# Both heads' scores in one tile of two PSUM banks, in a three-layer transformer kernel

## The chip, the cores and the metric

The kernel runs on one core of a Trainium2 chip. The metric is device time in microseconds. The engines are PE (matrix products; PEld is its weight load), DVE (vector), ACT (activation function), POOL (general) and SP (here only DMA issue). PSUM, into which PE writes, has eight banks of 128 x 512 fp32 values.

## The reference

The sequence has 512 positions of 1024 channels, fp32 throughout. `reference()` runs one hybrid layer and then two further layers:

```python
# first layer: attention over a window of 128 with sinks, beside an RWKV7 recurrence
attn = sliding_window_sink_attention(q, k, v, rel_bias, sinks[l])
rw = rwkv7_time_mix(p, ...)                      # state per head, 64 x 64, step by step
x = x + rms_norm(concat([attn, rw]) @ w_out[l], ...)
x = x + rms_norm(conv_gated_ffn(...), ...)
# second layer (even): fox (scores plus a decay) and diff (p1 - lam * p2), 8 and 2 x 4 heads of 64
s = einsum('bqhd,bkhd->bhqk', qb, k) * scale + (cb[..., :, None] - c[..., None, :])
p = softmax(where(qpos[:, None] >= kpos[None, :], s, -inf))
# third layer (odd): dsa (an indexer picks the top 128 keys of each row) and stick-breaking attention
a = where(mask, exp(log_sigmoid(z) + after), 0.0)  # after: sums of log(1 - sigmoid) from the right
# each layer ends with a gated FFN with a short convolution
```

## The kernel before, in words

Activations stay on the chip, channels on partitions. A dense projection is one PSUM tile of 128 x 512. Every weight tile and every input is split into a high and a low part, and a product takes three matmuls for each 128 input channels (lines 222 to 224), 24 in a row for 1024 channels. `Stream` brings the weights by DMA from SP in units of 512 KB, and ACT and DVE split them (lines 335, 336).

The program has six stages: the first mixer (0 to about 440 us), its FFN (to 985), the even layer (to 1290), its FFN (to 1646), the odd layer (to 1946) and its FFN.

In the first mixer the string `CFG["order"]` lists the steps. D projects r, k and v of two heads, A makes the operands of the recurrence's chunks (lines 547 to 642: two low-rank products 553 and 560, then blocks of 64-row matmuls 620 and 621, transposes, and 638), I inverts a triangular system on DVE, J joins its quarters (683, 693), B runs the eight chunks one after the other (713 to 787), S is the window attention of one pair of heads (799 to 854), Q projects its queries, and F is the output projection. Each is there for j = 0 to 3. These chains share PE's queue with dense projections.

The order of instructions on an engine is made by a scheduler that places an instruction when its inputs and its buffers are free; the text order counts among those that share a buffer. A PSUM bank is taken with `bank(tag)` from a pool, new for each use: two of `q` (dense), two of `s`, one each of `b`, `n`, `a` and `o`. Dense tiles use `q`, and after the mixer (`spread`) every third one `b`. In the mixer A uses `s`, J and B use `b` (for j = 3 `s`), S uses `a`, and outputs of B and S collect in `o` or `n`. Later, transposes alternate between `n` and `a`, and scores use `s`.

In the even and odd layers a step is one pair of heads j and one block of 128 queries b, with n = 128 (b + 1) keys. Each head in turn takes a bank `s`, gets its score matmul (1130 in fox, 1169 in diff, 1302 in stick, 1327 in dsa) from one half of the 128 rows of the two heads' queries and keys, in fox a 32-row matmul for the decay (1131), and a mask added by a product with the identity. DVE reduces the maximum (1135, 1172, 1331), ACT exponentiates, PE transposes block by block (1000) into a bank that DVE or ACT copies out (1003, 1005), and `values` (1012) multiplies by v. In stick ACT takes two sigmoids, DVE scans and POOL multiplies (1309). The indexer's four heads (1248) are summed after a relu.

Of the kernel before, what the change touches and what calls it, by code (L numbers as in the profile page):

```python
# [22 lines left out]
P = 128  # L23
# [18 lines left out]
M3 = {"ot": 4, "pre": 2, "rtmp": 1, "isc": 3, "irl": 2, "selb": 3, "kf": 4, "vd": 4, "PT": 3,  # L42
      "sq": 1, "sk": 1, "svt": 2, "e": 4, "sg": 2, "sc": 2, "cq": 4, "w3": 3}
# [3 lines left out]
BANKS = dict(q=2, s=2, b=1, n=1, a=1, o=1)  # L47
# [18 lines left out]
class K:  # L66
    def __init__(self, tc, ctx, dbg):
        self.tc, self.nc, self.dbg = tc, tc.nc, dbg or {}
        self.c = ctx.enter_context(tc.tile_pool(name="cst", bufs=1))
        self.xp = ctx.enter_context(tc.tile_pool(name="xp", bufs=1))  # L70
        self.w = ctx.enter_context(tc.tile_pool(name="w", bufs=1))
        self.ps = ctx.enter_context(tc.tile_pool(name="ps", bufs=1, space=PSUM))
        self.dr = ctx.enter_context(tc.tile_pool(name="dr", bufs=1, space=DRAM))
        self.n = self.nq = self.nt = 0
        self.spread = False
# [18 lines left out]
    def bank(self, tag):  # L94
        self.n += 1
        return self.ps.tile([P, S], F32, name=f"{tag}_{self.n}", tag=tag, bufs=BANKS[tag])

    def psq(self):
        self.nq += 1
        return self.bank("b" if self.spread and self.nq % 3 == 0 else "q")  # L100

    def pss(self):
        return self.bank("s")

    def pstr(self, tag="tr"):
        if tag == "tr":
            self.nt += 1
            tag = "na"[self.nt % 2]
        return self.bank(tag)
# [341 lines left out]
def first_mixer(k, I):  # L451
# [51 lines left out]
    def swa_table():  # L503
# [3 lines left out]
        q = k.pstr("a")  # L507
# [473 lines left out]

def rows_T(k, p, b, i, tag="pT"):
    nc = k.nc
    q = k.pstr()
    for kb in range(b + 1):
        nc.tensor.transpose(q[:, kb * P:(kb + 1) * P], p[:, kb * P:(kb + 1) * P], k.ident)
    t = k.slot(tag)
    n = (b + 1) * P
    if i % 2:
        nc.vector.tensor_copy(t[:, :n], q[:, :n])  # L990
    else:
        nc.scalar.activation(t[:, :n], q[:, :n], AF.Copy)
    return t
# [49 lines left out]
def even_layer(k, I, x, h, st, bc, q):  # L1043
# [68 lines left out]
    def fox_proj(j):  # L1112
        qt = evac(k, k.proj(st, h), "aq", bc, 0.125)
        kt = evac(k, k.proj(st, h), "ak", bc)
# [3 lines left out]
    def fox(j, qt, kt, vt):  # L1118
        ls8 = k.small("ls8", 8)
        pts = [k.slot("PT", (P, 13, P)) for _ in range(2)]  # L1120
        for b in range(NB):
            for hh in range(2):
                hd = 2 * j + hh
                hs = slice(64 * hh, 64 * hh + 64)
                g, i = divmod(hd, 4)
                n = (b + 1) * P
                ex = [(CL[g][32 * i:32 * i + 32, b * P:(b + 1) * P], CR[g][32 * i:32 * i + 32, :n], 0),
                      (k.identb, k.causb, b * P)]
                q = k.pss()
                nc.tensor.matmul(q[:, :n], qt[hs, b * P:(b + 1) * P], kt[hs, :n], start=True, stop=False)  # L1130
                nc.tensor.matmul(q[:, :n], ex[0][0], ex[0][1], start=False, stop=False, tile_position=(32 * i, 0))
# [5 lines left out]
                nc.scalar.activation(p[:, :n], q[:, :n], AF.Exp, bias=nm, accum_out=ls8[:, u:u + 1])  # L1137
# [22 lines left out]
    def diff(j, qt, kt, vt):  # L1160
        ls1 = k.small("ls1", 4)
        o = k.pso()
        for b in range(NB):
            n = (b + 1) * P
            ps, l12 = [], k.small("l12", 2)
            for hh in range(2):
                hs = slice(64 * hh, 64 * hh + 64)
                q = k.pss()
                nc.tensor.matmul(q[:, :n], qt[hs, b * P:(b + 1) * P], kt[hs, :n], start=True, stop=False)  # L1169
                nc.tensor.matmul(q[:, b * P:n], k.identb, k.causb, start=False, stop=True)  # L1170
                nm = k.small("nm", 1)
                nc.vector.tensor_reduce(nm, q[:, :n], axis=AX.X, op=OP.max, negate=True)
                p = k.slot("p")
                nc.scalar.activation(p[:, :n], q[:, :n], AF.Exp, bias=nm,
# [32 lines left out]
    prev = None  # L1207
    for j in range(4):
        cur = fox_proj(j)
# [14 lines left out]
def odd_layer(k, I, x):  # L1224
# [17 lines left out]
    for b in range(1, NB):  # L1242
        n = (b + 1) * P
        sc = k.slot("isc")
        for i in range(4):
            hs = slice(64 * (i % 2), 64 * (i % 2) + 64)
            q = k.pss()
            nc.tensor.matmul(q[:, :n], iq[i // 2][hs, b * P:(b + 1) * P], ikd[hs, :n], start=True, stop=True)
            rl = k.slot("irl")
            nc.scalar.activation(rl[:, :n], q[:, :n], AF.Relu)  # L1250
            if i == 0:
                nc.vector.tensor_scalar(sc[:, :n], rl[:, :n], iw[:, 4 * b:4 * b + 1], None, op0=OP.mult)
            else:
                nc.vector.scalar_tensor_tensor(sc[:, :n], rl[:, :n], iw[:, 4 * b + i:4 * b + i + 1], sc[:, :n], op0=OP.mult, op1=OP.add)
# [40 lines left out]
    def stick(j, qt, kt, vt):  # L1295
        pts = [k.slot("PT", (P, 13, P)) for _ in range(2)]
        for b in range(NB):
            n = (b + 1) * P
            for hh in range(2):
                hs = slice(64 * hh, 64 * hh + 64)  # L1300
                q = k.pss()
                nc.tensor.matmul(q[:, :n], qt[hs, b * P:(b + 1) * P], kt[hs, :n], start=True, stop=False)
                nc.tensor.matmul(q[:, b * P:n], k.identb, k.strictb, start=False, stop=True)
                a, r = k.slot("e"), k.slot("sg")
                nc.scalar.activation(a[:, :n], q[:, :n], AF.Sigmoid)
                nc.scalar.activation(r[:, :n], q[:, :n], AF.Sigmoid, scale=-1.0)
                c = k.slot("sc")
                nc.vector.tensor_tensor_scan(c[:, n - 2::-1], r[:, n - 1:0:-1], r[:, n - 1:0:-1], 1.0, op0=OP.mult, op1=OP.min)  # L1308
                nc.gpsimd.tensor_tensor(a[:, :n - 1], a[:, :n - 1], c[:, :n - 1], op=OP.mult)
                u = 2 * b + hh  # L1310
                put_T(k, a, b, u, pts[hh])
# [6 lines left out]
    def dsa(j, qt):  # L1318
# [3 lines left out]
        for b in range(NB):  # L1322
            for hh in range(2):
                hs = slice(64 * hh, 64 * hh + 64)
                n = (b + 1) * P
                q = k.pss()
                nc.tensor.matmul(q[:, :n], qt[hs, b * P:(b + 1) * P], kt[hs, :n], start=True, stop=False)  # L1327
                nc.tensor.matmul(q[:, :n], k.identb, k.causb if b == 0 else sel[b][:, :n], start=False, stop=True)
                u = 2 * b + hh
                nm = k.small("nm", 1)  # L1330
                nc.vector.tensor_reduce(nm, q[:, :n], axis=AX.X, op=OP.max, negate=True)
                p = k.slot("e")
                nc.scalar.activation(p[:, :n], q[:, :n], AF.Exp, bias=nm, accum_out=ls8[:, u:u + 1])
                put_T(k, p, b, u, pts[hh])
# [54 lines left out]
def net(ctx, tc, I, out, dbg=None, stages=(1, 2, 3)):  # L1389
# [19 lines left out]
    if 2 in stages:  # L1409
        with k.phase("m2", M2):  # L1410
            even_layer(k, I, x, h, st, bc, q)
        with k.phase("f2", F2):
            ffn2(k, I, x, 0)
    if 3 in stages:
        with k.phase("m3", M3):
            odd_layer(k, I, x)
        with k.phase("f3", F2):
# [149 lines left out]
```

## Time and profile before

| | |
|---|---|
| median of 3 runs | 2326.16 us (2322.17 to 2332.09) |
| profiled execution | 2324.15 us |
| its span | 2322.1 us |
| PE busy | 2259.6 us, 97% |
| DVE busy | 1429.0 us, 62% |
| ACT busy | 924.9 us, 40% |
| mean granted clock of PE | 0.984 |

The span is the time from the first to the last instruction of the profiled execution. A matmul's recorded end is modelled, and successive ones overlap, so the distance between two starts tells more than the duration of one. A share of busy time is an average over stages that differ.

### The profile page before, as it was taken

To read this page: it belongs to the slowest core of one execution; us is meant where nothing else is said; L and a number is where in the kernel's file an instruction comes from. 1 tells how busy PE (TensorE), PEld (TensorE's weight loads), DVE (VectorE), ACT (ScalarE), POOL (GpSimd) and SP (SyncE) were. 2 spreads that over 40 slices of the span, in tenths; PEclk is the share of its full clock that TensorE was granted. 3 is DMA by queue.
4 is the path that set the end of the run, shared out by engine and by line. 5 is a ranking of instruction groups with operands and counts; after the bars stand their busy time and mean duration, and the time that the engine had idled before them with its cause. 6 is when DMAs were issued, how large, how long until landed. Compare 5 with 4: busy or idle time off the path is not lost.

```text
span 2322.1 us, 30329 instructions
## 1 busy us (share of the span) xinstructions
PE 2259.6 (97%) x11784; PEld 1778.8 (77%) x11784; DVE 1429.0 (62%) x2597; ACT 924.9 (40%) x1533; POOL 343.7 (15%) x327
## 2 busy tenths in 40 slices
PE   8899998999999999999999999999999999999998
PEld 6677677888888889966667888888756658888888
DVE  5978764766436666543676662564696646653665
ACT  4234423544324444343344442443343444433443
POOL 2111101411001113200111111111012202111111
PEclk9989979999999999999999999999999999999999
DMA  5111112132332335311112323333211102323334
GB/s 164 59 35 36 28 50 68 57 106 94 105 96 95 100 109 173 121 37 46 55 46 74 99 94 97 100 95 97 83 46 40 52 19 91 96 95 100 97 113 154
DMA packets 66304, 192.83 MB, mean 83 GB/s; under 512 B 15808, under 2 KB 19152, under 8 KB 66160
## 3 DMA queue, kind: packets, MB, share of 16 engines
q1 hardware_dynamic: 65584, 189.70, 25.5%
q0 software_dynamic: 576, 1.19, 0.3%
q8 instruction: 92, 1.51, 0.3%
q14 instruction: 52, 0.43, 0.1%
HBM read 188.24 MB, written 2.63 MB: 82 GB/s over the span
## 4 chain that ended last, share of the span: by engine, by line
PE 86%; DVE 9%; ACT 2%; issue 2%; POOL 2%; DMA 0%; SPq 0%; DVEq 0%; POOLq 0%; ACTq 0%
PE q L222 16%; PE q L224 16%; PE q L223 15%; PE b L224 7%; PE b L222 7%; PE b L223 7%; PE o L1012 2%; DVE invm L650 1%; DVE wl L336 1%; PE s L1327 1%; PE s L1130 1%; PE s L1169 1%; DVE sc L1308 1%; PE a L813 1%; POOL nsq L163 1%
## 5 line engine op out<-in xcount | busy, mean ns | idle before, releaser
L336 DVE TENSOR_TENSOR wl<-raw,wh 128x1024 fp32r<-128x1024 f32 x341 | 433.5, 1272 | 261.7 <-ACT wh L335 259.9
L335 ACT ACTIVATE wh<-raw 128x1024 fp32r<-128x1024 f32 x341 | 359.7, 1055 | 463.7 <-PE q L223 252.5
L222 PE MATMUL q<-hh,wh 128*128 128x512 f32 (+1 forms) x1294 | 512.8, 397 | 9.8 <-ACT hh L190 7.4
L224 PE MATMUL q<-hh,wl 128*128 128x512 f32 (+1 forms) x1294 | 513.6, 397 | 0.3 <-DVE wl L336 0.2
L223 PE MATMUL q<-hl,wh 128*128 128x512 f32 (+1 forms) x1294 | 511.9, 396 | 0.6 <-DVE hl L191 0.5
L222 PEld LDWEIGHTS q<-hh,wh 128*128 128x128 f32 x1294 | 247.1, 191 | 61.7 <-ACT hh L190 7.8
L223 PEld LDWEIGHTS q<-hl,wh 128*128 128x128 f32 x1294 | 247.8, 191 | 53.2 <-issue 5.4
L224 PEld LDWEIGHTS q<-hh,wl 128*128 128x128 f32 x1294 | 247.4, 191 | 52.2 <-issue 4.5
L223 PE MATMUL b<-hl,wh 128*128 128x512 f32 (+1 forms) x602 | 233.8, 388 | 0.0
L224 PE MATMUL b<-hh,wl 128*128 128x512 f32 (+1 forms) x602 | 232.0, 385 | 0.0
L222 PE MATMUL b<-hh,wh 128*128 128x512 f32 (+1 forms) x602 | 231.5, 385 | 0.0
L273 POOL TENSOR_TENSOR zu<-za,z 128x512 f32<-128x512 f32 x76 | 101.0, 1328 | 815.2 <-DVE z L268 758.5
L222 PE MATMUL q<-gh,wh 128*128 128x256 f32 (+1 forms) x559 | 189.2, 338 | 1.8 <-ACT gh L130 1.0
L224 PE MATMUL q<-gh,wl 128*128 128x256 f32 (+1 forms) x559 | 188.9, 338 | 2.1 <-DVE wl L336 2.1
L223 PE MATMUL q<-gl,wh 128*128 128x256 f32 (+1 forms) x559 | 187.6, 336 | 0.0
L130 ACT ACTIVATE gh<-zu 128x512 fp32r<-128x512 f32 x76 | 48.1, 632 | 250.9 <-POOL zu L273 250.8
L131 DVE TENSOR_TENSOR gl<-zu,gh 128x512 fp32r<-128x512 f32 x76 | 52.6, 692 | 151.2 <-ACT gh L130 151.2
L266 ACT ACTIVATE z<-u,pv 128x512 f32<-128x512 f32 x152 | 122.7, 810 | 31.2 <-DVE u L265 31.2
L163 POOL TENSOR_TENSOR nsq<-nsq,nsq 128x256 f32<-128x256 f32 (+1 forms) x84 | 96.9, 1155 | 244.8 <-ACT nsq L158 244.5
L223 PEld LDWEIGHTS b<-hl,wh 128*128 128x128 f32 x602 | 113.9, 189 | 23.4 <-issue 2.2
L224 PEld LDWEIGHTS b<-hh,wl 128*128 128x128 f32 x602 | 113.9, 189 | 23.1 <-issue 1.7
L222 PEld LDWEIGHTS b<-hh,wh 128*128 128x128 f32 x602 | 113.9, 189 | 22.3 <-issue 0.9
(555 smaller groups left out, 3472.9 us busy)
## 6 DMA issues: line engine op xcount, KB each, us to landing
raw<-in_ffn_up SPq DMA_DIRECT2D x88, 512.0 KB, 3.4
raw<-in_w_ffn_up SPq DMA_DIRECT2D x64, 512.0 KB, 3.4
raw<-in_ffn_down SPq DMA_DIRECT2D x55, 512.0 KB, 3.4
raw<-in_w_ffn_down SPq DMA_DIRECT2D x48, 512.0 KB, 3.5
raw<-in_ev_w_in SPq DMA_DIRECT2D x24, 512.0 KB, 3.4
raw<-in_w_in SPq DMA_DIRECT2D x20, 512.0 KB, 3.7
raw<-in_od_w_in SPq DMA_DIRECT2D x20, 512.0 KB, 3.4
x<-in_x SPq DMA_DIRECT2D x16, 256.0 KB, 4.0
```

The source lines that it names most:

```text
L130: nc.scalar.activation(hi, x, AF.Copy)
L131: nc.vector.tensor_tensor(lo, x, hi.bitcast(F32), op=OP.subtract)
L163: (nc.gpsimd if m % chains == 0 else nc.vector).tensor_tensor(acc, acc, sq, op=OP.add)
L222: nc.tensor.matmul(o, wh, xh, start=(k == 0), stop=False)
L223: nc.tensor.matmul(o, wh, xl, start=False, stop=False)
L224: nc.tensor.matmul(o, wl, xh, start=False, stop=(k == n - 1))
L266: nc.scalar.activation(y, v, AF.Identity, bias=col(3), scale=col(2))
L273: nc.gpsimd.tensor_tensor(u, a, z[1], op=OP.mult)
L335: nc.scalar.activation(a, part, AF.Copy)
L336: (nc.gpsimd if self.pool > 0 else nc.vector).tensor_tensor(b, part, a.bitcast(F32), op=OP.subtract)
L650: nc.vector.transpose(out=M[32 * g:32 * g + 32], in_=R[j]["aab"][32 * g:32 * g + 32, :, 32 * i:32 * i + 32] .rearrange("r u c -> r c u")[: ...
L1012: k.nc.tensor.matmul(o[64 * hh:64 * hh + 64, kb * P:], v(kb, hh), pts[hh][:, 4 * kb:3 * kb + NB].rearrange("p c t -> p (c t)"), start=(kb ...
```

## The change

Four of the eight banks become two fixed tiles of two banks each, `pairs[0]` and `pairs[1]`. What used to take a bank `s` takes the halves of `pairs[0]` in turn; what used to take `a` or `b` takes the first or second half of `pairs[1]`. In the even and odd layers (`held`) dense tiles use the two `q` only and transposes the one `n`, and a step takes one of the two tiles in turn by `pair()`: both heads' score matmuls are issued side by side into its two banks, then both masks, and one reduction reads both. In stick the scan works in place, the sigmoids and the indexer's relu read both heads, and in fox the queries and keys of j = 1 are projected ahead of the step j = 0.

```diff
-BANKS = dict(q=2, s=2, b=1, n=1, a=1, o=1)
+BANKS = dict(q=2, n=1, o=1)
+PAIRS = 2
...
+        self.pairs = [self.ps.tile([P, 2, S], F32, name=f"s{i}") for i in range(PAIRS)]
+        self.held = False
...
     def bank(self, tag):
+        if tag == "s":
+            return self.pss()
+        if PAIRS == 2 and tag in "ab":
+            return self.pairs[1][:, "ab".index(tag)]
...
     def psq(self):
-        return self.bank("b" if self.spread and self.nq % 3 == 0 else "q")
+        return self.bank("b" if self.spread and not self.held and self.nq % 3 == 0 else "q")
     def pss(self):
-        return self.bank("s")
+        self.ns += 1
+        return self.pairs[0][:, self.ns % 2]
+    def pair(self):
+        self.ns += 1
+        return self.pairs[self.ns % PAIRS]
     def pstr(self, tag="tr"):
...
-            tag = "na"[self.nt % 2]
+            tag = "n" if self.held else "na"[self.nt % 2]
...
+def scores(k, qq, qt, kt, b, alone=False):
+    n = (b + 1) * P
+    for hh in range(2):
+        hs = slice(64 * hh, 64 * hh + 64)
+        k.nc.tensor.matmul(qq[:, hh, :n], qt[hs, b * P:(b + 1) * P], kt[hs, :n], start=True, stop=alone)
+def masks(k, qq, mask, at, n):
+    for hh in range(2):
+        k.nc.tensor.matmul(qq[:, hh, at:n], k.identb, mask, start=False, stop=True)
...
         for b in range(NB):                       # diff; fox and dsa alike
+            qq = k.pair()
+            scores(k, qq, qt, kt, b)
+            masks(k, qq, k.causb, b * P, n)
+            nm = k.small("nm", 2)
+            nc.vector.tensor_reduce(nm, qq[:, :, :n], axis=AX.X, op=OP.max, negate=True)
             for hh in range(2):
-                q = k.pss()
-                nc.tensor.matmul(q[:, :n], qt[hs, b * P:(b + 1) * P], kt[hs, :n], start=True, stop=False)
-                nc.tensor.matmul(q[:, b * P:n], k.identb, k.causb, start=False, stop=True)
-                nm = k.small("nm", 1)
-                nc.vector.tensor_reduce(nm, q[:, :n], axis=AX.X, op=OP.max, negate=True)
                 p = k.slot("p")
-                nc.scalar.activation(p[:, :n], q[:, :n], AF.Exp, bias=nm,
+                nc.scalar.activation(p[:, :n], qq[:, hh, :n], AF.Exp, bias=nm[:, hh:hh + 1],
```

Three places of PE's order follow. In the rows of the changed kernel `s_69` is `pairs[0]` and `s_70` is `pairs[1]`, whichever half is meant, and its lines up to 980 stand 12 further down (S0 begins with line 811 in place of 799).

First place, the start of S0 in the first mixer. Before, it stands among the projections of D, with bank `a`:

```order
L224 MATMUL q_1398<-hh_121,wl_1402 128x512
L222 MATMUL q_1398<-hh_123,wh_1401 128x512
L223 MATMUL q_1398<-hl_124,wh_1401 128x512
L224 MATMUL q_1398<-hh_123,wl_1402 128x512
L799 MATMUL a_1434<-sws_1431,J_407 128x512
L222 MATMUL q_1548<-hh_109,wh_1551 128x512
```

In the changed kernel line 799 is the last matmul of B0, on the same tile as the first of S0 (811):

```order
L236 MATMUL q_2403<-hh_113,wl_2407 128x512
L234 MATMUL q_2403<-hh_115,wh_2406 128x512
L799 MATMUL s_70<-sg_416,gup_382 128x512
L610 MATMUL s_69<-t_229_1677,blk_56_384 128x512
L235 MATMUL q_2403<-hl_116,wh_2406 128x512
L811 MATMUL s_70<-sws_1384,J_404 128x512
```

S0 moved from before the whole of J0 and B0 (rows 444 to 634 of the kernel before) to directly behind it.

Second place, the end of B1. Before, its last matmul is line 787, and S2 (813, 832, 837) runs beside it with dense matmuls between:

```order
L782 MATMUL b_2281<-ident,xc_2257 128x128 x4
L813 MATMUL a_2366<-swk_443,swq_1429 128x256
L224 MATMUL q_2523<-hh_119,wl_2527 128x512
L222 MATMUL q_2523<-hh_121,wh_2526 128x512
L787 MATMUL b_2289<-sg_419,gup_384 128x512
L832 MATMUL a_2376<-ident,sws_2337 128x128 x4
L223 MATMUL q_2523<-hl_122,wh_2526 128x512
```

In the changed kernel:

```order
L777 MATMUL n_2062<-vt_1011,x_962 64x64
L794 MATMUL s_70<-ident,xc_2155 128x128 x4
L591 MATMUL s_69<-ident,kti_2584 128x128 x4
L799 MATMUL s_70<-sg_416,gup_382 128x512
L610 MATMUL s_69<-t_348_2595,blk_56_384 128x512
L811 MATMUL s_70<-sws_2188,J_404 128x512
L632 MATMUL s_69<-ar_2591,ksq_2559 64x128
L633 MATMUL s_69<-ar_2591,kti_2599 64x128
```

S2 (811) now begins behind B1, with steps of A3 on the other tile beside it, and the dense matmuls are gone from there.

Third place, fox, j = 0, the block with 384 keys. Before, the heads follow each other whole:

```order
L1000 MATMUL n_8932<-ident,p_8930 128x128 x2
L1130 MATMUL s_8948<-ak_8888,aq_8886 128x384
L1000 MATMUL a_8944<-ident,p_8942 128x128 x2
L1131 MATMUL s_8948<-cT_8848,cT_8841 128x384
L1132 LDWEIGHTS identb
L1132 MATMUL s_8948<-causb,identb 128x128
L1130 MATMUL s_8961<-ak_8888,aq_8886 128x384
```

In the changed kernel, where 998 is the score matmul, 1154 the decay, 254 the transposition of v and 1024 that of a block of probabilities:

```order
L998 MATMUL s_69<-ak_8668,aq_8666 128x384
L254 MATMUL n_8672<-ident,av_8670 128x128 x4
L998 MATMUL s_69<-ak_8668,aq_8666 128x384
L1154 MATMUL s_69<-cT_8628,cT_8621 128x384
L1024 MATMUL n_8696<-ident,p_8694 128x128
L1154 MATMUL s_69<-cT_8628,cT_8621 128x384
```

The two heads' matmuls are closer, but here a transposition stands between those of each kind; a pair with nothing between reads `x2`.

## Rows read from the trace of the kernel before

**Rows 1.** The page's busy shares: busy us, share of the span, instructions.

```profile
PE 2259.6 (97%) x11784; PEld 1778.8 (77%) x11784; DVE 1429.0 (62%) x2597; ACT 924.9 (40%) x1533; POOL 343.7 (15%) x327
```

**Rows 2.** Windows by stage: length, busy time per engine, granted clock, DMA.

```profile
core 0: us, PE busy (x) PEld busy (x) DVE busy (x) ACT busy (x) POOL busy (x), PEclk, DMA share, GB/s
0.00:440.00 440.00, 407.33 (x2910) 315.25 (x2911) 306.51 (x851) 166.12 (x346) 82.69 (x99) 0.93 0.20 61
...
985.00:1290.00 305.00, 300.86 (x1357) 205.96 (x1356) 175.78 (x383) 114.25 (x265) 25.23 (x22) 1.00 0.17 54
...
1646.00:1946.00 300.00, 289.82 (x1246) 185.52 (x1246) 206.20 (x385) 120.43 (x250) 50.66 (x49) 1.00 0.14 46
```

**Rows 3.** The same view of the first mixer, cut finer.

```profile
110.00:187.00 77.00, 73.62 (x582) 55.27 (x580) 59.63 (x186) 25.86 (x60) 7.64 (x8) 0.91 0.15 39
187.00:305.00 118.00, 114.72 (x992) 85.38 (x991) 96.33 (x285) 50.89 (x134) 17.78 (x18) 0.97 0.10 26
305.00:347.00 42.00, 41.28 (x213) 31.04 (x213) 23.49 (x88) 9.26 (x13) 1.52 (x2) 0.72 0.21 60
347.00:382.00 35.00, 34.58 (x353) 27.30 (x352) 13.29 (x33) 11.22 (x24) 0.00 (x0) 1.00 0.27 88
382.00:440.00 58.00, 47.35 (x295) 42.26 (x294) 37.93 (x100) 25.47 (x55) 30.37 (x38) 0.88 0.14 45
```

**Rows 4.** Single lines of the mixer: ns min/median/max, first and last start.

```profile
L799 PE MATMUL a<-sws,J x8: 591/592/697, 109.7 to 268.1; 128*128 128x512 f32 x8
...
L854 PE MATMUL a<-ident,swp x16: 270/273/329, 179.1 to 304.1; 128*128 128x128 f32 x16
...
L683 PE MATMUL s<-rq,aab x32: 191/191/212, 347.0 to 349.7; 32*32 32x32 f32 x32
...
L787 PE MATMUL b<-sg,gup x6: 591/592/697, 184.5 to 341.0; 128*128 128x512 f32 x6
...
L787 PE MATMUL s<-sg,gup x2: 592/594/595, 381.4 to 381.8; 128*128 128x512 f32 x2
```

**Rows 5.** Timeline of PE: start us, us, instruction; diff, then the indexer.

```profile
1128.49 0.39 PE L224 MATMUL q<-hh,wl 128*128 128x512 f32 x1
1128.72 0.40 PE L222 MATMUL q<-hh,wh 128*128 128x512 f32 x1
...
1129.49 1.12 PE L1169 MATMUL s<-ak,aq 64*128 64x512 f32 x2
1130.55 0.23 PE L1170 MATMUL s<-causb,identb 128*128 128x128 bf16 x1
...
1659.81 0.70 PE L1248 MATMUL s<-kf,kf 64*128 64x256 f32 x4 [0.52 <-DVE kf L963]
```

**Rows 6.** Groups by shape: score and decay matmuls, even layer, then the indexer's.

```profile
L1130 PE MATMUL s<-ak,aq 64*128 64x512 f32 x16 | 9.0, 641 | 0.0
...
L1131 PE MATMUL s<-cT,cT 32*128 32x512 f32 x8 | 4.0, 494 | 0.0
...
L1130 PE MATMUL s<-ak,aq 64*128 64x128 f32 x16 | 3.9, 322 | 0.0
...
L1131 PE MATMUL s<-cT,cT 32*128 32x128 f32 x8 | 2.6, 322 | 0.0
...
L1248 PE MATMUL s<-kf,kf 64*128 64x384 f32 x8 | 2.5, 535 | 0.3 <-ACT irl L1250 0.3
```

**Rows 7.** Groups of DVE's lines in the even layer.

```profile
L1135 DVE TENSOR_REDUCE nm<-s 128x1 f32<-128x128 f32 (+3 forms) x32 | 15.6, 490 | 27.5 <-PE s L1132 23.1 <-ACT PT L1005 3.5 <-ACT p L1137 0.5
...
L1003 DVE COPY PT<-a 128x128 f32<-128x128 f32 (+3 forms) x16 | 7.8, 489 | 6.7 <-PE a L1000 6.2
```

**Rows 8.** PE's waits in the even, then the odd layer: us, times, longest.

```profile
PE n L1197 <- DVE on L1194: 3.6, 4, 1.1
...
PE a L1000 <- POOL e L1309: 4.7, 8, 1.1
PE n L1000 <- POOL e L1309: 3.6, 8, 0.8
```

More of the change, by code (lines that the diff above doesn't have):

```diff
@@ L1165, in diff @@
             ps, l12 = [], k.small("l12", 2)
-            for hh in range(2):
[L1167 to L1172, printed above, removed]
+            qq = k.pair()
+            scores(k, qq, qt, kt, b)
+            masks(k, qq, k.causb, b * P, n)
+            nm = k.small("nm", 2)
+            nc.vector.tensor_reduce(nm, qq[:, :, :n], axis=AX.X, op=OP.max, negate=True)
+            for hh in range(2):
                 p = k.slot("p")
-                nc.scalar.activation(p[:, :n], q[:, :n], AF.Exp, bias=nm,
+                nc.scalar.activation(p[:, :n], qq[:, hh, :n], AF.Exp, bias=nm[:, hh:hh + 1],
                                      accum_out=(ls1[:, b:b + 1] if hh == 0 else l12[:, 1:2]))
@@ L1205, in diff @@
             oT[4 + j] = hi, lo
-    prev = None
-    for j in range(4):
-        cur = fox_proj(j)
+    cur = fox_proj(0)
+    qk = fox_qk(1)
+    fox(0, *cur)
+    for j in range(1, 4):
+        cur = fox_proj(j, qk)
+        qk = None
         fox(j, *cur)
@@ L1245, in odd_layer @@
         for i in range(4):
[L1246 to L1250, printed above, removed]
+            if i % 2 == 0:
+                qq, rl = k.pair(), k.slot("irl", (P, 2, S))
+                scores(k, qq, iq[i // 2], ikd, b, True)
+                nc.scalar.activation(rl[:, :, :n], qq[:, :, :n], AF.Relu)
+            r, w = rl[:, i % 2, :n], iw[:, 4 * b + i:4 * b + i + 1]
             if i == 0:
-                nc.vector.tensor_scalar(sc[:, :n], rl[:, :n], iw[:, 4 * b:4 * b + 1], None, op0=OP.mult)
+                nc.vector.tensor_scalar(sc[:, :n], r, w, None, op0=OP.mult)
             else:
-                nc.vector.scalar_tensor_tensor(sc[:, :n], rl[:, :n], iw[:, 4 * b + i:4 * b + i + 1], sc[:, :n], op0=OP.mult, op1=OP.add)
+                nc.vector.scalar_tensor_tensor(sc[:, :n], r, w, sc[:, :n], op0=OP.mult, op1=OP.add)
         nc.vector.tensor_tensor(sc[:, b * P:n], sc[:, b * P:n], k.caus, op=OP.add)
@@ L1298, in stick @@
             n = (b + 1) * P
-            for hh in range(2):
[L1300 to L1311, printed above, removed]
+            qq = k.pair()
+            scores(k, qq, qt, kt, b)
+            masks(k, qq, k.strictb, b * P, n)
+            a, r = k.slot("e", (P, 2, S)), k.slot("sg", (P, 2, S))
+            nc.scalar.activation(a[:, :, :n], qq[:, :, :n], AF.Sigmoid)
+            nc.scalar.activation(r[:, :, :n], qq[:, :, :n], AF.Sigmoid, scale=-1.0)
+            for hh in range(2):
+                back = r[:, hh, n - 1:0:-1]
+                nc.vector.tensor_tensor_scan(back, back, back, 1.0, op0=OP.mult, op1=OP.min)
+                nc.gpsimd.tensor_tensor(a[:, hh, :n - 1], a[:, hh, :n - 1], r[:, hh, 1:n], op=OP.mult)
+                put_T(k, a[:, hh], b, 2 * b + hh, pts[hh])
         o = values(k, pts, lambda kb, hh: vt[:, kb * P + 64 * hh:kb * P + 64 * hh + 64])
@@ L1322, in dsa @@
         for b in range(NB):
-            for hh in range(2):
[L1324 to L1328, printed above, removed]
-                u = 2 * b + hh
[L1330 to L1334, printed above, removed]
+            n = (b + 1) * P
+            qq = k.pair()
+            scores(k, qq, qt, kt, b)
+            masks(k, qq, sel[b][:, :n] if b else k.causb, 0, n)
+            nm = k.small("nm", 2)
+            nc.vector.tensor_reduce(nm, qq[:, :, :n], axis=AX.X, op=OP.max, negate=True)
+            p = k.slot("e", (P, 2, S))
+            for hh in range(2):
+                u = 2 * b + hh
+                nc.scalar.activation(p[:, hh, :n], qq[:, hh, :n], AF.Exp, bias=nm[:, hh:hh + 1], accum_out=ls8[:, u:u + 1])
+                put_T(k, p[:, hh], b, u, pts[hh])
         o = values(k, pts, lambda kb, hh: vd[kb][:, (2 * j + hh) * 64:(2 * j + hh + 1) * 64])
@@ L1410, in net @@
         with k.phase("m2", M2):
+            k.held = True
             even_layer(k, I, x, h, st, bc, q)
+            k.held = False
         with k.phase("f2", F2):
@@ L1415, in net @@
         with k.phase("m3", M3):
+            k.held = True
             odd_layer(k, I, x)
+            k.held = False
         with k.phase("f3", F2):
```

28 lines of the change are left out of this document (14 added, 14 removed).

## The prediction

> **What bounds the kernel now.** I read the page's busy shares first, then windows cut at the layers, the first mixer cut finer, when single lines of it run, then the groups of lines, and the waits. PE is busy 2259.6 of 2322.1 us [rows 1], so a change pays by taking time from PE's queue and costs by leaving PE without work. The stages differ. The even layer (985 to 1290) has 300.9 of 305 us busy, the odd layer (1646 to 1946) 289.8 of 300, and the first mixer (0 to 440) only 407.3 of 440, with a granted clock of 0.93 where those layers have 1.00 [rows 2]. In the first mixer dense projections fill PE's queue between the links of long dependent chains, so that from 110 to 305 PE shows only 77.0 - 73.6 + 118.0 - 114.7 = 6.7 us idle [rows 3]. In the two attention layers it is idle for 4 and 10 us, 3.6 of it behind one line of diff and 4.7 + 3.6 on POOL's product in stick [rows 2, 8].
>
> **What the change removes in the attention layers.** One head's score matmul contracts over 64 rows. At the largest size its two passes start at 1129.49 and the mask after them at 1130.55, 1.06 us for a head [rows 5]. One pass is recorded at 641 ns, 0.11 us more than half of 1.06. At 128 columns it is recorded at 322 [rows 6]; less 0.11 and doubled, 0.42 us a head. The two sizes between go evenly: 0.63 and 0.85. Two heads on opposite halves of the rows can run together: in the indexer four passes of 256 columns, two heads, take 0.70 us in all [rows 5], where one head's two take 0.63. So a pair that stands side by side costs one head, not two.
>
> By the order, of 64 pairs (fox, diff, stick, dsa: 16 each) only 32 have their two matmuls next to each other; in the others the transposes or a projection's transposition stand between the two heads, as in the third place of the section on the change. They are 13 at 128 columns, 8 at 256, 5 at 384 and 6 at 512: 13 x 0.42 + 8 x 0.63 + 5 x 0.85 + 6 x 1.06 = 21.1 us. The 32-row decay matmul of fox is one pass, recorded at 322 to 494 ns [rows 6], so 0.21 to 0.38 us; the four sizes sum to 1.19 us. Fox has four pairs of each size, so at most 4.8 us are saved, and with 14 of the 16 pairs adjacent 4.2 us. The indexer's pairs already overlap (2.5 us busy for eight passes of 535 ns [rows 6]), so I count nothing for it. Sum for both layers: -25 us if PE never waits more than now.
>
> The Trainium skill, page "TensorEngine Tiling (Array Packing)", section "Key Properties", says that changing the tiling mode drains the engine. That speaks for counting a pair with a 128-row transpose inside as no pair. By that rule the sum is the 25 us above; without it, and with all 64 pairs together, it would be the rival below. No row here shows such a broken pair.
>
> The rest of these edits lies off PE's path. Reductions for the maximum fall from 96 to 48 calls (32 in each of three blocks; 15.6 us of DVE in fox [rows 7]), but each of the new ones reads both heads, and DVE has 175.8 of 305 us busy [rows 2]; I count nothing, at most -3 us where a reduction is the last thing before an exponential. The merged sigmoids and the scan in place sit in the stretch where PE already waits 8.3 us for POOL [rows 8]; between -8 and +5, taken as nothing.
>
> **What it adds there.** The transposes of a head lose one of two banks, the dense tiles one of three. A transposition must now wait for the copy of the one before: by the nearest row such a copy takes 489 ns on DVE [rows 7]. There are 32 of them in fox, 16 in diff, 64 in stick and dsa, 112 in all: between 0 (dense matmuls stand between them; one follows the other every 0.23 us [rows 5], two cover a copy) and 112 x 0.49 = 55 us. In the order most neighbours have dense matmuls or a pair between, so I take a tenth, 5 us. **Even and odd layer together: -20 us**, between -33 and +30.
>
> **What it adds in the first mixer.** This is the larger term. Before, S (window attention) works through bank a, J and B (the recurrence) through bank b, A through two banks s, each handed out apart. Now a and b are the two halves of one tile and both s banks are the halves of the other, and the order shows that each tile is one thing to wait for: the first matmul of S0 stands directly behind the last of B0 and waits for DVE, which reads B0's last result; before, it stood far ahead of B0's end, at 109.7 us [rows 4]. So S and B alternate in program order: J0, B0, S0, J1, S1, B1, S2, J2, S3, B2. The dense work doesn't wait for them and goes ahead: between the first matmul of S0 and the last of S3 the order has 186 dense matmuls before and 34 after. The whole of J1, S1 and B1 has six.
>
> The chain then sets the end of B3. B0 ends at about 186 before (its last matmul begins at 184.5 [rows 4]); in the new order it has two dense tiles more in front of it (48 x 0.23 = 11 us [rows 5]) and no S0 beside it (a part of which stood between), so I put its end at 188. From there: S0 beside the rest of A2, then S1, J1 and B1, S2 beside the rest of A3, S3, J2 and B2, J3 and B3. What each takes: J3 and B3 ran from 347.0 to 382 before, 35 us, in a window with few dense matmuls [rows 3, 4], so 35 for J1 and B1; the later two have the output projection between their links (it is what is left of the dense work), 40 and 38. S3 ran from 268.1 to 304.4 with dense work and a stage A beside it, 36 us [rows 4]; beside A alone I take 34, since in the new order A's use of a half also waits for the reader of the other half, and with nothing beside it 24 (an estimate: two thirds of the 36, as PE's queue then makes no link wait). Sum: 34 + 24 + 35 + 34 + 24 + 40 + 38 = 229, so B3 ends at 188 + 229 = 417 where it ended at 382: +35 us. Behind it the order has 297 dense matmuls before the next FFN's, and 248 before; 49 x 0.23 = 11 us, of which the 10.6 idle us of 382 to 440 [rows 3] take half: +5. I take **+40 us**. Bounds: with every piece short (24, 18, 30, 24, 18, 30, 30 = 174) B3 would end at 362, and then PE's queue decides, not the chain: 0. With S as long as it was seen, beside A 45, and B at 38 to 42 (45 + 36 + 38 + 45 + 36 + 42 + 42 = 284), +95. The clock belongs to that end: from 305 to 347, with few matmuls, the records show 0.72 granted against 0.97 in 187 to 305 [rows 3], a mean over the two levels of 1.2 and 2.4 GHz; a chain of waits could get as little.
>
> The FFN stages keep their three dense banks, with one of them in the shared tile: nothing, between -2 and +4. Outside the span nothing changes.
>
> **Sum.** The profiled execution took 2324.15 us for a span of 2322.1, 2 us below the median 2326.16. 2324 - 20 + 40 = 2344, so 2346 against the median: slower by 0.9%.
>
> **Rivals.**
> *The mixer hides it.* The chains S and B have slack: the last dense work must follow them all the same, and the moved matmuls only change places. For it: in 382 to 440 PE is idle 10.6 of 58 us, so the end of the mixer isn't paced by PE alone; against it: PE shows 6.7 idle us between 110 and 305 [rows 3], so there is little from which a gap could be paid. Then the first mixer costs 0 to +10 and the time is 2326 + 5 - 25 = 2306, faster. Chance 0.20.
> *All pairs overlap.* If a transpose between two heads breaks nothing, the saving is that of 64 pairs: 16 x (0.42 + 0.63 + 0.85 + 1.06) + 4.8 = 52 us, and with +40 in the mixer the time is 2326 + 40 - 52 = 2314. Faster; against it, PE takes instructions in order and the head behind the transpose can't start beside the one before. Chance 0.05.
> *The two cancel.* With +25 and -25: 2326, no change. Chance 0.12.
> *The single transposition bank decides.* If half of the 112 handovers wait for a copy, 27 us, and the saving is spent: the attention layers cost +2, the mixer +40: 2368, slower. Price per handover 0.49; from some 50 waiting handovers on it outweighs the pairs. For it: fox's reductions and copies share DVE and ACT with the weight splits; against it: PE idles only 4 us in the even layer now [rows 2]. Chance 0.15.
>
> **How the numbers follow.** A change of 0.5% (12 us) is about what can be told from none. Forecast (slower by 12 to 40): 0.48. Slower by more (the last rival, or the mixer's upper bound): 0.15. No change: 0.12. Faster: 0.20 + 0.05 = 0.25. The range takes in the first rival's 2306, the last one's 2368 and, of the mixer's upper bound, what lies within 20 us beyond it: 2304 to 2390. The forecast alone: 2338 to 2366.
>
> **What would show it.** Right: the windows of the first mixer lengthen, with more idle PE between the first S0 matmul (now near 190 us, not 110) and the last of S3, and B3 ends near 417; PE's waits there name DVE and ACT on the s tiles. The 512-column pairs that are adjacent take 1.06 us, the broken ones 2.1. PE's idle time in the even and odd layers grows by no more than 5 us, and these layers shorten by about 20. Wrong: an unchanged end of the mixer near 440, S0 ahead of B0 in time, or broken pairs that overlap.

## The result, and the profile after

The changed kernel takes 2402.39 us (2395.41 to 2407.38, 4 runs) against 2327.24 (now 4 runs): slower by a factor of 1.032 (95% interval 1.028 to 1.036), 75 us where 20 were forecast. The direction was right, the size wrong, and the time lies above the range. Executions of the kernel before lie between 2320 and 2349 us, the longest with a mean granted clock of 0.971 where the profiled one had 0.984, so the time of a single run below is read only together with its trace. The profiled execution of the changed kernel took 2399.31 us, with a span of 2397.4. The page's busy shares, and PE's clock in 40 slices of the span, in tenths of full speed:

```profile
PE 2290.9 (96%) x11784; PEld 1803.5 (75%) x11784; DVE 1419.0 (59%) x2549; ACT 915.2 (38%) x1495; POOL 343.5 (14%) x327
...
PEclk9998556989999999999999999999999999999999
```

The number of matmuls is the same as in [rows 1]. The fifth to seventh slice, 240 to 420 us, have a clock of 0.5 to 0.6.

To see where the time went I cut each trace at four marks: the first product of the first FFN on DVE (the mixer's end), the first of the second FFN, the last addition of that FFN, and the first product of the third. These pieces begin and end a little apart from the stages of [rows 2]. The pieces in us (the first FFN and the even layer stand together, since some kernels below move work across their boundary):

| | mixer | FFN and even | FFN | odd | FFN | 
|---|---|---|---|---|---|
| before | 439.6 | 849.8 | 346.1 | 324.8 | 361.8 |
| after | 528.5 | 835.0 | 346.1 | 324.4 | 363.4 |
| difference | +88.9 | -14.8 | 0 | -0.4 | +1.6 |

So the mixer lost 89 us and the even layer gave 15. In the mixer, these windows answer to [rows 3] (length, busy time by engine, clock):

```profile
187.00:305.00 118.00, 96.56 (x587) 69.38 (x585) 60.41 (x187) 31.25 (x81) 11.06 (x12) 0.65 0.07 18
305.00:382.00 77.00, 65.74 (x297) 43.36 (x298) 43.97 (x145) 19.39 (x54) 6.87 (x6) 0.54 0.02 4
382.00:440.00 58.00, 53.75 (x489) 42.21 (x488) 18.27 (x57) 16.69 (x41) 2.42 (x3) 0.84 0.15 42
```

From 187 to 305 PE runs 587 matmuls where it ran 992, and at 0.65 of the clock where it had 0.97. Single lines (ns min/median/max, first and last start), S's first and last and B's last matmul, answer to [rows 4]:

```profile
L811 PE MATMUL s<-sws,J x8: 592/697/1220, 192.9 to 358.4; 128*128 128x512 f32 x8
...
L866 PE MATMUL s<-ident,swp x16: 421/421/474, 222.6 to 393.9; 128*128 128x128 f32 x16
...
L799 PE MATMUL s<-sg,gup x8: 592/592/1219, 190.5 to 460.3; 128*128 128x512 f32 x8
```

S0 begins at 192.9 instead of 109.7, and the last S ends at 394 instead of 304. The same 128x128 transpose has a median of 421 ns where it had 273, and single 128x512 matmuls take 1220 where they took 592: the lower of the two clock levels. PE's waits between 187 and 440 (us, times, longest) are many small ones:

```profile
PE o L849 <- ACT swp L846: 9.5, 13, 1.0
PE s L794 <- DVE xc L791: 6.5, 2, 6.3
PE s L825 <- DVE sws L826: 4.3, 7, 0.7
PE s L844 <- ACT sws L834: 4.1, 2, 2.2
```

They are links of S and B that dense work used to cover; none is longer than 6.3 us.

In the even layer the pairs do what was forecast. The timeline of PE shows a pair that stands side by side, and one with a transpose (1024) inside:

```profile
1143.30 1.13 PE L998 MATMUL s<-ak,aq 64*128 64x512 f32 x4
1144.85 0.33 PE L1024 MATMUL n<-ident,p 128*128 128x128 f32 x1 [0.43 <-ACT p L1162]
...
1101.06 1.12 PE L998 MATMUL s<-ak,aq 64*128 64x512 f32 x2
1102.12 0.33 PE L1024 MATMUL n<-ident,p 128*128 128x128 f32 x1
1102.38 1.12 PE L998 MATMUL s<-ak,aq 64*128 64x512 f32 x2
1103.43 0.44 PE L1024 MATMUL n<-ident,p 128*128 128x128 f32 x2
```

Four passes, two heads, take 1.13 us when adjacent. With one transpose between them they take from 1101.06 to 1103.43, 2.37 us: 1.06 for the first head, 0.26 for the transpose and 1.05 for the second head, so the heads run one after the other, as in [rows 5].

In the odd layer PE has less to do and waits more. Windows of the even and the odd layer, before and after, then waits of PE in the odd one:

```profile
965.00:1289.00 324.00, 319.86 (x1501) 224.22 (x1500) 186.42 (x411) 120.60 (x278) 32.99 (x35) 1.00 0.17 54
1635.00:1960.00 325.00, 314.77 (x1368) 206.23 (x1367) 215.15 (x405) 126.30 (x257) 50.66 (x49) 1.00 0.16 52
```

```profile
1054.00:1363.00 309.00, 301.33 (x1502) 215.32 (x1501) 181.28 (x379) 117.48 (x278) 34.48 (x35) 1.00 0.18 57
1709.00:2034.00 325.00, 309.62 (x1369) 205.21 (x1368) 209.39 (x389) 119.79 (x219) 48.69 (x49) 0.98 0.17 53
```

```profile
PE n L1024 <- POOL e L1335: 6.4, 9, 1.3
PE n L161 <- DVE ry L155: 3.7, 2, 3.5
PE n L971 <- DVE pre L982: 1.6, 2, 1.4
...
PE n L1024 <- DVE PT L1027: 0.9, 1, 0.9
```

In the even layer PE's work falls by 18.5 us, and its idle time rises from 4 to 8. In the odd layer the work falls by 5, and the idle time rises from 10 to 15: what the pairs saved there is idle time now. The wait for POOL's product is not what grew, it fell from 8.3 [rows 8] to 6.4. New are 3.5 us before the norm's row (161), 15 us into the layer, 1.4 before a rotation (971), and 0.9 for a copy out of the single transposition bank.

### The profile page after: what moved, and what is told of

Its sections match the earlier page's. It is cut to its first block, busy times and chain, and to the rows that moved or that the text cites. A ratio compares the mean times of both kernels' runs of the same rounds, so it can differ in the third digit from the quotient of the medians.

```text
span 2397.4 us, 30207 instructions
## 1 busy us (share of the span) xinstructions
PE 2290.9 (96%) x11784; PEld 1803.5 (75%) x11784; DVE 1419.0 (59%) x2549; ACT 915.2 (38%) x1495; POOL 343.5 (14%) x327
## 4 chain that ended last, share of the span: by engine, by line
PE 84%; DVE 10%; ACT 2%; issue 2%; POOL 2%; DMA 0%; SPq 0%; DVEq 0%; ACTq 0%; POOLq 0%
PE q L234 16%; PE q L235 16%; PE q L236 16%; PE s L234 6%; PE s L235 6%; PE s L236 6%; PE s L998 2%; DVE wl L348 2%; PE o L1036 2%; PE n L1024 1%; DVE invm L662 1%; PE s L825 1%; ACT wh L347 1%; PE o L849 1%; POOL nsq L175 1%
## 5 line engine op out<-in xcount | busy, mean ns | idle before, releaser
L234 PE MATMUL q<-hh,wh 128*128 128x512 f32 (+1 forms) x1438 | 570.4, 397 | 7.7 <-ACT hh L202 7.7
L235 PE MATMUL q<-hl,wh 128*128 128x512 f32 (+1 forms) x1438 | 569.3, 396 | 0.5 <-DVE hl L203 0.5
L236 PE MATMUL q<-hh,wl 128*128 128x512 f32 (+1 forms) x1438 | 568.4, 395 | 0.2 <-DVE wl L348 0.2
L234 PEld LDWEIGHTS q<-hh,wh 128*128 128x128 f32 x1438 | 273.8, 191 | 69.9 <-issue 9.1
L234 PE MATMUL s<-hh,wh 128*128 128x512 f32 (+1 forms) x482 | 184.4, 383 | 0.0
L236 PE MATMUL s<-hh,wl 128*128 128x512 f32 (+1 forms) x482 | 184.1, 382 | 0.0
L235 PE MATMUL s<-hl,wh 128*128 128x512 f32 (+1 forms) x482 | 183.8, 381 | 0.0
L280 DVE SCALAR_TENSOR_TENSOR z<-u,pv,z 128x510 f32<-128x510 f32 x152 | 115.8, 764 | 4.9
L234 PEld LDWEIGHTS q<-gh,wh 128*128 128x128 f32 x559 | 106.4, 190 | 14.4 <-ACT wh L347 2.7
L236 PEld LDWEIGHTS q<-gh,wl 128*128 128x128 f32 x559 | 106.1, 190 | 13.8 <-DVE wl L348 1.9
```

The costliest lines, as they stand in the source:

```text
L234: nc.tensor.matmul(o, wh, xh, start=(k == 0), stop=False)
L235: nc.tensor.matmul(o, wh, xl, start=False, stop=False)
L236: nc.tensor.matmul(o, wl, xh, start=False, stop=(k == n - 1))
L280: nc.vector.scalar_tensor_tensor(y[:, 2:], v[:, :S - 2], col(0), y[:, 2:], op0=OP.mult, op1=OP.add)
```

## The experiments

A cut of an edit has `...` where lines are left out. Theory A: the mixer lost its time because banks of two chains became halves of one tile, which the program tracks as one buffer. Rival B: fixed tiles in place of banks handed out anew cost the time, whoever shares them. Theory C: the low clock is a cause of its own; rival D: only a symptom. Pieces of all runs, cut as above:

| | mixer | FFN and even | odd | time, us |
|---|---|---|---|---|
| e1_chain_tiles | 458.0 | 837.4 | 325.2 | 2328.87, ratio 1.0007 (0.9986 to 1.0027) |
| e2_s_shared | 481.8 | 838.5 | 324.3 | 2357.62, one run |
| e3_before_ab | 508.7 | 853.9 | 328.9 | 2401.76, one run |
| e4_fill | 509.6 | 837.5 | 324.4 | 2381.43, one run |
| e5_fill_long | 504.0 | 838.7 | 326.1 | 2379.84, one run |
| e6_one_pair_ss | 466.8 | 831.1 | 339.2 | 2347.05, ratio 1.0115 (1.0027 to 1.0203) |
| e7_one_pair_ao | 440.8 | 837.0 | 358.8 | 2347.58, ratio 1.0081 (1.0048 to 1.0113) |
| e8_adjacent | 462.8 | 820.9 | 318.1 | 2315.33, one run |
| e9_best | 441.7 | 826.8 | 319.3 | 2297.67, ratio 0.9872 (0.9838 to 0.9905) |
| e10_best_unpaired | 445.3 | 826.4 | 324.5 | 2305.83, one run |

The eighth has the first's order of S, J and B in the mixer and ends it 5 us later; the tenth ends it 4 us behind the ninth in the same way. Differences of 5 us in the mixer are not read.

**Whose halves share a tile.**

```diff
-CFG = {... 'ob': 'onno', ...}                         # bank of B's output, by j
+CFG = {... 'ob': 'nnno', ...}
...
-BANKS = dict(q=2, n=1, o=1)
+BANKS = dict(q=2)
+HALF = dict(b=(0, 0), n=(0, 1), a=(1, 0), o=(1, 1))   # tile, half
...
+        self.single = [self.ps.tile([P, S], F32, name=f"t{i}") for i in range(2)]   # s; n and o while held
...
```

Two norms are given bank n or a by name as well, here and in the second, seventh, eighth, ninth and tenth experiments, and `ob` is the same in all of these.

> The changed kernel with the halves of the two tiles given to one chain each: b with n (both the recurrence's) and a with o (both the window attention's), and two single banks for s. In the attention layers nothing else changes: the two single banks take the parts of n and o. Theory A (the mixer's loss comes from the tile that S and B share and the one that A's steps share): S0 begins near 110 us again, the granted clock between 187 and 305 goes back to some 0.95, the mixer ends at 440 to 450 instead of 528, and the time is 2327 - 15 + 5, some 2317 us. Rival B (fixed tiles, whoever shares them, cost the time, since the scheduler no longer hands banks out): the mixer still ends beyond 500 and the time stays above 2380.

S's first matmul, and the window:

```profile
L817 PE MATMUL s<-sws,J x8: 591/592/697, 110.9 to 270.6; 128*128 128x512 f32 x8
```

```profile
187.00:305.00 118.00, 113.18 (x805) 82.05 (x806) 81.64 (x249) 42.82 (x112) 17.57 (x19) 0.81 0.09 21
```

S0 begins at 110.9, and 70 of the 89 us are back, with all of the mixer's banks a, b, n, o still halves of fixed tiles. Rival B falls as an account of most of the loss. The expectation missed on the rest: the mixer ends at 458, not 440 to 450, and the clock is 0.81. The clock of one window in one execution says little by itself: the eighth experiment runs the same order there at 0.97 and ends the mixer 5 us later. Whether the remaining 18 us come from the tile of b and n or from the two fixed banks for s was not tried; the seventh experiment clears the tile of a and o.

**The s tile alone in addition.**

```diff
-BANKS = dict(q=2, n=1, o=1)
+BANKS = dict(q=2, a=1, o=1)
...
-        if PAIRS == 2 and tag in "ab":
-            return self.pairs[1][:, "ab".index(tag)]
+        if tag in "bn":
+            return self.pairs[1][:, "bn".index(tag)]
...
```

> The changed kernel with b and n in one tile and a and o single, but the two s banks still halves of one tile. Theory A1 (the tile of a and b carries nearly all of the loss): the mixer ends within 10 us of the first experiment's, since only A's steps wait for each other (A0 took 36 us before and 44 in the changed kernel, and two such steps stand on the path). Rival A2 (A's own serialisation carries half of it): the mixer ends 30 us or more behind the first experiment's, near 480.

The mixer ends 24 us behind the first experiment's: between the two expectations. A's steps, which wait for each other's readers, cost more than A1 had it.

**The a and b tile alone, in the kernel before.**

```diff
-BANKS = dict(q=2, s=2, b=1, n=1, a=1, o=1)
+BANKS = dict(q=2, s=2, n=1, o=1)
...
+        self.both = self.ps.tile([P, 2, S], F32, name="both")
...
+        if tag in "ab":                               # in bank()
+            return self.both[:, "ab".index(tag)]
...
-        q = k.pstr("a")                               # in the table of S's bias
+        q = k.pss()
```

> The kernel before with one thing changed: a and b are halves of one fixed tile; scores, dense banks and transposes stay as they were. Theory A1: the mixer alone reproduces most of the loss, with S0 near 190 us and the mixer's end at 500 to 530; the even and odd layers may lose a few us more, as their transposes and dense tiles share that tile. Rival: without the s tile shared the chains still overlap enough, and the mixer ends below 470.

S's first matmul, then two windows:

```profile
L802 PE MATMUL both<-sws,J x8: 592/645/1061, 185.3 to 347.3; 128*128 128x512 f32 x8
```

```profile
187.00:305.00 118.00, 95.64 (x602) 68.19 (x601) 65.42 (x202) 30.96 (x82) 12.67 (x13) 0.68 0.07 18
305.00:382.00 77.00, 64.61 (x335) 46.67 (x336) 42.24 (x139) 23.27 (x64) 3.93 (x4) 0.60 0.03 6
```

One shared tile, with nothing else of the change, makes the mixer 69 us longer, delays S0 to 185 and brings the clock down to 0.68 and 0.60. With the 27 us that the shared s tile costs by itself (sixth experiment) the two make 96, and 89 together: that is theory A, with its parts.

**Work that nobody reads.**

```diff
-CFG = {'order': '... B3 r0 r2 r3 F', ...}
+CFG = {'order': '... B3 X0 r0 r2 r3 F', ...}
...
+        elif o == "X":
+            for _ in range(20):                       # 40 in the longer one
+                q = k.psq()
+                for _ in range(2):
+                    nc.tensor.matmul(q, k.ident, DP[3][0], start=True, stop=True)
```

> The changed kernel with 40 extra matmuls of 128x512 fp32 in the mixer, whose results nobody reads, in the gaps of PE's order while S and B alternate; at the full clock they are 42 us of added PE work. Theory C (half of the loss is the clock: the chain runs with a granted clock of 0.5 to 0.65 and its matmuls take up to twice as long): the clock between 187 and 382 rises above 0.8, S1 and B1 shorten from 30 and 47 us towards 24 and 37, and the mixer ends no later than 528, perhaps at 510, though PE does more. Rival D (the chain waits for DVE and ACT, the clock is a mere symptom): the mixer ends 15 to 40 us later than 528.

> The changed kernel with 80 unread matmuls in the mixer where the fourth experiment had 40, so that they last until about S3's start instead of running out in B1. In the fourth experiment the clock was 0.99 between 187 and 305, where fill lay, and 0.66 between 305 and 382, where it had run out, and the next FFN's gate matmul came 19 us earlier than in the changed kernel. Theory C (the clock is a cause): between 305 and 382 the clock rises above 0.85 as well, S2 and S3 shorten, and the gate matmul comes another 5 to 20 us earlier, near 1020 us, where it was 965 before. Rival D (the gain came from something else that the first 40 moved): no further gain, or a loss of up to 40 us for the added work.

Windows of the shorter fill, of the longer, the longer's first matmuls of S and last of B, and the gate matmul behind the first FFN (451) in the shorter and the longer:

```profile
187.00:305.00 118.00, 112.19 (x696) 67.30 (x694) 72.19 (x227) 32.74 (x84) 14.08 (x14) 0.99 0.08 22
305.00:382.00 77.00, 64.12 (x347) 44.93 (x346) 43.26 (x142) 23.96 (x65) 4.80 (x5) 0.66 0.03 6
```

```profile
187.00:305.00 118.00, 114.39 (x698) 67.32 (x696) 72.15 (x224) 32.87 (x84) 14.86 (x15) 1.00 0.08 21
305.00:382.00 77.00, 75.55 (x535) 45.05 (x535) 44.15 (x143) 25.91 (x76) 4.15 (x5) 1.00 0.04 8
382.00:440.00 58.00, 57.87 (x473) 44.58 (x473) 23.29 (x62) 14.43 (x27) 2.77 (x3) 1.00 0.19 64
```

```profile
L811 PE MATMUL s<-sws,J x8: 592/592/697, 194.9 to 340.9; 128*128 128x512 f32 x8
...
L799 PE MATMUL s<-sg,gup x8: 592/592/697, 192.5 to 431.2; 128*128 128x512 f32 x8
```

```profile
L451 PE MATMUL s<-hh,wz x16: 283/283/283, 1034.9 to 1047.1; 128*128 128x256 f32 x16
...
L451 PE MATMUL s<-hh,wz x16: 283/283/283, 1032.0 to 1044.3; 128*128 128x256 f32 x16
```

PE does more, and the mixer is shorter by 19 and by 24.5 us: theory C, and rival D falls. Where fill lies the clock is 0.99 or 1.00, where it has run out 0.66. B1's last matmul ends 37 to 38 us after S1's end, where the changed kernel takes 47; S1 itself goes from 30 us to 28, not towards 24. Nearly all of the gain comes from the first 40. The second 40 brought the clock between 305 and 382 to 1.00, as expected, but the mixer's end only 5.6 us forward, and the gate matmul 2.9 (1034.9 to 1032.0) where 5 to 20 were expected: that part is not clear of the 5 us that are not read here. What is left with the clock at 1.00 from 187 to 440, 64 us, is the order's own, with the fill's work in it.

**One pair tile, of two choices.** The sixth is the changed kernel with `PAIRS = 1`, banks a and b single and `held` never set. The seventh gives the one tile to a and o:

```diff
-BANKS = dict(q=2, n=1, o=1)
-PAIRS = 2
+BANKS = dict(q=2, s=2, b=1, n=1)
+PAIRS = 1
...
+        if tag in "ao":
+            return self.pairs[0][:, "ao".index(tag)]
...
-            tag = "n" if self.held else "na"[self.nt % 2]
+            tag = ("nb" if self.both else "nn" if self.held else "na")[self.nt % 2]
...
-        return self.bank("o")
+        return self.bank("s" if self.held else "o")
...
```

> Only the first half of the change: one tile of two banks (the halves serve as the two s banks), with a and b single banks as before, three dense banks and two transposition banks in the attention layers. Theory A: the mixer loses only what A's steps lose by the shared s tile, 15 to 35 us (between the first experiment's +18 at the mixer's end and the second's +42). In the attention layers all pairs but a few are adjacent in the order (65 of 70), so up to 45 us could go, but a pair must wait until both exponentials of the pair before have read the tile: I expect the even layer at 300 to 315 us (324 before, 309 in the changed kernel). Time about 2340. Rival: the single pair tile stalls PE and the even layer is no shorter than 324.

> One tile of two banks, whose halves are a and o of the mixer, both the window attention's own, and all other banks single as before; in the attention layers two dense banks and one shared one, two transposition banks, and the pairs take turns on the one tile. Theory A: nothing in the mixer waits for another chain's reader, so it ends at 440 to 450 us, with S0 near 110. The even layer as in the sixth experiment. Time 2300 to 2315, faster than before. Rival B (fixed tiles cost by themselves): the mixer ends at 458 or later, as in the first experiment.

The seventh's S and B, its waits in the odd layer, and that layer's window:

```profile
L808 PE MATMUL s<-sws,J x8: 591/592/1222, 108.3 to 269.9; 128*128 128x512 f32 x8
...
L796 PE MATMUL b<-sg,gup x6: 591/592/697, 183.4 to 339.7; 128*128 128x512 f32 x6
```

```profile
PE n L1021 <- ACT e L1355: 10.3, 6, 2.2
PE n L1021 <- POOL e L1333: 9.9, 15, 1.4
PE b L1021 <- POOL e L1333: 9.3, 14, 1.9
PE b L1021 <- ACT e L1355: 6.5, 4, 2.2
```

```profile
1637.00:1996.00 359.00, 317.88 (x1356) 207.02 (x1359) 219.08 (x395) 126.47 (x224) 57.49 (x51) 0.92 0.14 46
```

S and B run as in [rows 4], and the mixer ends at 440.8: this fixed tile, whose halves belong to one chain, costs nothing, and rival B falls for it. The time missed the expectation by 30 us and more, since it had not asked what one pair at a time does to the odd layer. There PE waits 36 us for POOL's products and ACT's exponentials, the clock falls to 0.92, and the layer is 34 us longer than before. That the wait comes from scores that can't be made ahead is argued; with a second pair tile the tenth experiment takes 324.5 there. The sixth, also with one pair at a time, is only 14 us longer in the odd layer; the two differ as well in the banks of dense tiles, transposes and values, and what of the 34 is due to these was not tried. In the even layer, with dense projections to run meanwhile, one tile is enough. The sixth ends the mixer at 466.8: the shared s tile costs 27 us.

**Adjacency.** On the first experiment's kernel, in `scores`:

```diff
+        with k.tc.high_priority(40):
             k.nc.tensor.matmul(qq[:, hh, :n], qt[hs, b * P:(b + 1) * P], kt[hs, :n], start=True, stop=alone)
```

> The first experiment's kernel with the two score matmuls of a pair given priority, so that 58 of 70 pairs (indexer's included) stand adjacent in the order instead of 39. Theory (a pair costs one head only when nothing stands between): the 19 further pairs, most of 384 and 512 columns, save some 17 us of PE: the even layer goes from 322.6 to some 315, the odd layer from 325 to some 316. Rival (PE isn't what sets the odd layer's time, it is the scan and the selection on DVE): the odd layer stays at 325.

The FFN and even layer fall by 16.5 us to 820.9 and the odd layer by 7.1 to 318.1: 24 us, more than the 17 expected of the score matmuls alone (fox's decay matmuls and masks move closer too; that part isn't separated). The odd layer's rival falls. The whole time is 2315.33 in its one run, 13.5 us below the first experiment's median: its mixer ended 5 us later, and the first's profiled run was 4 us above that median.

**What they point to.** One tile of a and o up to the second FFN; then the pool of s, b and n is closed, and a second pair tile is opened with a transposition bank and one for the values:

```diff
...
+    def second(self):
+        self.px.close()
+        self.ps1 = self.px.enter_context(self.tc.tile_pool(name="ps2", bufs=1, space=PSUM))
+        self.pairs.append(self.ps1.tile([P, 2, S], F32, name="p1"))
...
```

> What the experiments point to, put together. Mixer, first two FFNs and even layer: one tile of a and o, which cost the mixer nothing in the seventh experiment (440.8 us, 439.6 before), other banks single; even layer with three dense banks, two transposition banks and one pair at a time. From the odd layer on, where one pair at a time cost 34 us, two pair tiles, and priority for a pair's two score matmuls as in the eighth, where the odd layer went to 318. By these: mixer and FFN 966 (965 before), even layer 305 to 311 (324), odd layer 318 (325), sum 2322 - 13 to 19 - 7: a time of 2298 to 2306, faster by 0.8 to 1.2%. Rival: the banks that change hands between the FFN and the odd layer make PE wait there, and the odd layer takes back what it gains.

> The ninth without the priority for a pair's matmuls: in the order 47 of 70 pairs stand adjacent instead of 60. The mixer and the even layer as in the ninth; the odd layer some 6 us longer, near 324, if adjacency is what shortens it there.

S's first matmul, and the even and odd layer's windows in the ninth:

```profile
L816 PE MATMUL p<-sws,J x8: 591/592/1222, 109.1 to 270.8; 128*128 128x512 f32 x8
```

```profile
966.00:1270.00 304.00, 293.75 (x1522) 211.98 (x1521) 185.73 (x384) 118.97 (x284) 33.78 (x36) 1.00 0.17 58
...
1618.00:1940.00 322.00, 304.41 (x1378) 202.17 (x1378) 212.49 (x395) 123.12 (x222) 54.11 (x49) 0.97 0.15 50
```

2297.67 us (6 runs), faster than the kernel before by 1.3% (0.95 to 1.62%), just below the time expected; the odd layer gave 5.5 us where 7 were counted, so the rival took little. Without the priority the odd layer is 5 us longer, as expected to within 1 us; 50 pairs of 70 stand adjacent in its order, not the 47 that the expectation says.

## Why the prediction was right, and where it was wrong

**The pairs.** Right, by mechanism and by price. An adjacent pair costs one head at each size (first passes of the two heads 6 to 7 ns apart; 0.42, 0.63, 0.85 and 1.06 us to the next start where nothing waits), and a broken one pays both heads and the transpose between. The trace has 32 of the 64 pairs adjacent, as the order said.

**The even and odd layers, -20.** They gave 15.2 in all, 14.8 of it in the even layer. PE's work fell by 23.7 us, close to the 25 of the sum. Its idle time grew by 8.7, where the sum had 5 for handovers and the sign of being right allowed 5. That the total came near has some luck in it: little of the new idle time is a handover of the transposition bank (about 1 us in each layer); most is the norm's row and the rotations in the odd layer, which no term named.

**The mixer, +40: the term that failed.** The mechanism was right: S and B alternate on the shared tile (third experiment), S0 begins at 192.9 (190 was said), and the dense work goes ahead. The size was 88.9. The step that failed is the chain from B0's end to B3's end: its pieces were added up to 229 us as if the clock stayed full, and it took 269. The pieces in us, from the first and last matmuls of the steps, beside those with the clock held up by the long fill:

| | put | changed kernel | long fill |
|---|---|---|---|
| S0 | 34 | 32 | 33 |
| S1 | 24 | 30 | 28 |
| J1 and B1 | 35 | 58 | 47 |
| S2 | 34 | 38 | 34 |
| S3 | 24 | 37 | 26 |
| J2 and B2 | 40 | 54 | 46 |
| J3 and B3 | 38 | 20 | 24 |
| sum | 229 | 269 | 238 |

The whole chain in the changed kernel and with the long fill, then the stretch behind B3 in the kernel before and in the changed one:

```profile
191.50:460.90 269.40, 232.36 (x1507) 167.53 (x1507) 128.52 (x402) 70.01 (x180) 20.36 (x22) 0.68 0.08 23
...
193.50:431.80 238.30, 233.28 (x1639) 145.74 (x1639) 129.40 (x401) 68.01 (x178) 20.51 (x22) 1.00 0.08 24
```

```profile
382.40:439.60 57.20, 46.55 (x292) 41.76 (x292) 37.53 (x100) 25.13 (x54) 29.97 (x38) 0.88 0.14 44
...
460.90:528.50 67.60, 55.80 (x341) 50.97 (x341) 41.00 (x104) 29.28 (x61) 27.76 (x38) 0.87 0.20 63
```

- The clock was left out of the sum. The 35 us for a J and a B came from a window at 1.00 [rows 3]; the chain ran at 0.68. The 0.72 of the same rows was named, but only beside the upper bound. With the clock at 1.00 the chain is 31 us shorter, though PE does the fill as well. Part of this returns behind B3, since 28 dense matmuls move there; at the mixer's end 24.5 us are left. With the short fill, which moves no dense matmul, the chain is 23 us shorter (246).
- At full clock the sum is 9 us too short. That it is so close is partly luck: J1 with B1 took 12 us more than put and J2 with B2 6, while J3 with B3 took 14 less, since it works on the other tile and overlaps B2.
- Behind B3 come 67.6 us, where 57.2 came before: +10, not +5. PE's work there grew by 9 us, near the 11 counted, but the idle time took up none of it: 11.8 us where it was 10.6.
- B0 ended at 191.5, 4 us later than put.

So of the 49 us missing, 40 are the chain, 5 the stretch behind it and 4 the start; half of the 49, 24.5 us, comes back at the mixer's end when the clock is held up.

**The range.** The upper bound of +95 in the mixer gives 2326 - 20 + 95 = 2401, the measured time, but the range was cut at 2390. The bound meets the number by luck: it had 38 for J1 and B1 and 42 for J3 and B3, which took 58 and 20.

**The rivals.** None came true: the mixer hid nothing, broken pairs did not overlap, the two terms did not cancel, and the single transposition bank decided nothing by itself.

## What to carry to other kernels

A buffer is what the scheduler tracks, so putting two banks into one tile joins the chains that use them. Give the halves to one chain, and read in the new order how much filler work is left between the links. When that filler goes, price the chain at the clock that the trace shows in stretches with few matmuls. And a pair is one only in the order: look for what the scheduler puts between its halves. If a bound that you worked out yourself is not refuted by a row, leave it inside the range.

## What was not expected of the hardware

Unread matmuls, up to 80 of 128x512 fp32, made the mixer 24 us shorter: with them the granted clock went from 0.65 and 0.54 to 1.00 in both stretches.

The price of a broken pair was not known, though its direction was forecast. A transpose between two 64-row matmuls undid their overlap in every broken pair: 1.94 us for 384 columns and 2.36 for 512 with one transpose between, where adjacent ones took 0.85 and 1.06. The Trainium skill, page "TensorEngine Tiling (Array Packing)", section "Key Properties", says that a change of the tiling mode drains the engine. The trace agrees as far as it goes: of four transposes between two heads, from 1098.43 us on, the later ones start 0.11 us apart, but the second starts 0.17 us after the first and the next head 0.20 us after the last. What else could take that time was not tried.
